# Neighbourhood attention with the two heads of a pair scored on the two row halves of TensorE, and a planner that groups by kind and knows PSUM banks

## The chip, the cores and the metric

The kernel runs on one core of one Trainium2 chip, in one launch. The metric is device time in microseconds (us). Three runs of the kernel before gave 2086.41, 2087.51 and 2084.97 us, a median of 2086.41.

## The reference, cut to what matters

Four layers work on 256 latent and 256 context tokens of width 1024. The layers' token mixers are grouped-query attention, neighbourhood attention, latent attention and grouped-query attention again; a SwiGLU feed-forward network with inner width 2816 follows each. All values are float32. The neighbourhood layer has 16 heads of 64 channels:

```python
q, k, v = jnp.split(t @ w_qkv, 3, axis=-1)          # shape (tokens, 16 heads, 64)
s_loc = einsum('bwhd,biwjhd->bhwij', qr, k_win) * scale + bias   # latent queries, latent keys in a window
s_ctx = einsum('bwhd,blhd->bhwl', qr, kc) * scale                # latent queries, all context keys
p = softmax(concatenate([s_loc, s_ctx], axis=-1))
o = einsum(p_loc, v_win) + einsum(p_ctx, vc)
oc = softmax_attend(qc, [kc], [vc], scale)          # context queries, context keys
```

Keys outside a window are masked by a bias of -1e30, so that all 256 latent keys are multiplied.

## The kernel before, in words

Every float32 product is made from float32r parts: an operand is split into a high part (ScalarE, ACT) and the rest (VectorE, DVE), and three TensorE matmuls add high*high, rest*high and high*rest into one PSUM bank. A weight piece of 128x1024 is loaded by SP, split into `whi` and `wlo`, and used. TensorE (PE) makes 128x512 or 128x256 outputs. PSUM has eight banks of 128x512, two for each of the tags `mm`, `sc`, `o` and `tp`.

Nothing is issued as it is written. Every call of the kernel is noted by `Planner.note` with a duration from `cost`; `schedule` then plays the program through in a list schedule, engine by engine, by due times from `backward`, and issues the instructions of the best of `PASSES` plans. So a planner's rule changes the order of the whole program. It knows the kind of a matmul, T (transpose), R (float32r) or F (other float32), and once it has issued a T it stays with T where it can.

In the neighbourhood layer (`attn_b`), `prep(c)` makes queries and keys of head pair c by two projections of 24 matmuls of 512 columns (tiles `m` = c and 8 + c, 128 channels = two heads), and for even c a quarter of the values. `stacked` takes each head apart: for a query, 64 rows of a tile `stk` hold the high part and the other 64 the rest; for a key, `stk` holds the high part in both halves and `stl` the rest in both. One head's scores are then two matmuls on all 128 rows, `ps<-stk` and `ps<-stl,stk`. That costs six ACT and six DVE instructions of 64x512 for a pair.

`head_units` gives three units for a head: context (`ca`: two blocks of 256 keys in one bank), and latent blocks 0 and 1 (`la`: 512 keys; the bias is added on DVE). A unit is scores, `softmax` (DVE maximum `nm`, ACT exponential `p`, DVE reciprocal `r`, POOL scaling `p`), then four transposes (`ps<-ident,p`) and their split (`pth`, `ptl`), then the product with `v`. `Pipe(2, 2)` sets these steps two units apart; `Stream` feeds the projections of the next pair between them.

`Norm.sums` makes the LayerNorm sums with 16 small F matmuls, each on 32 columns of the array (`ps<-zs,ones`, `ps<-x,ones`, `ps<-sq,ones`). `ada_first` and `ada_rest` multiply the modulation weights in the same way (`ps<-rawa,condp`).

Of the kernel before, what the change touches and what calls it, by code (L numbers as in the profile page):

```python
# [46 lines left out]
class Op:  # L47
    __slots__ = ("eng", "fn", "dur", "deps", "users", "tiles", "idx", "table", "left", "ready", "due", "start", "end",
                 "kind", "port", "rank", "pace")


class Planner:
# [9 lines left out]
    STAY = 1.5  # L62
    PASSES = 8
    PACE = 4.0
# [39 lines left out]
    def cost(self, queue, method, out, ins, k):  # L104
        n = 1
        for d in out.shape[1:]:
            n *= d
        if queue == "tensor":
            if method == "transpose":
                return 0.108  # L110
            if ins[0].dtype == F32R:
                return max(0.108, n / 2400.0 + 0.0133)
            return 0.083 if n <= 64 else 0.085 if n <= 128 else 0.242
        psum = any(x.space == bass.MemoryType.PSUM for x in ins)
        if queue == "sync":
            return n * out.shape[0] * 4 / 370e3
        n = max([n] + [self.width(x) for x in ins])
        extra = sum(self.width(x) == 1 for x in ins) + (k.get("accum_out") is not None)
        if queue == "scalar":
            return (0.05 if psum else 0.094) + n * 0.000835 + 0.093 * extra  # L120
        fast = method in ("tensor_scalar", "tensor_copy") and not psum
        if method == "reciprocal":
            return 0.07 + n * 0.0062
        if queue == "vector":
            return 0.07 + n * (0.00052 if fast else 0.00104) + 0.06 * extra
        if method == "tensor_scalar":
            return 0.115 + n * (0.00135 + 0.00035 * (len(ins) > 2))
        return 0.148 + n * 0.00217
# [18 lines left out]
    def note(self, queue, method, p, k):  # L147
# [16 lines left out]
        op.fn = lambda: getattr(getattr(self.nc, queue), method)(*p, **k)  # L164
        op.deps, op.users, op.tiles = set(), [], []
        for ap, w in [(x, False) for x in ins] + [(x, True) for x in outs]:
# [30 lines left out]
    def emit(self):  # L197
# [11 lines left out]
        for n in range(self.PASSES):  # L209
            self.backward(goal, aim)  # L210
            span = self.schedule()
            if best is None or span < best[0]:
                best = span, [o.start for o in self.ops]
            aim = [o.start if o.eng == "PE" else g for o, g in zip(self.ops, goal)]
        self.span, start = best
        for o in sorted(self.ops, key=lambda o: (start[o.idx], o.idx)):
            o.fn()
# [13 lines left out]
    def schedule(self):  # L231
# [15 lines left out]
        for o in ops:  # L247
            o.left = len(o.deps) + sum(slot[t] is None for t in o.tiles)
            o.ready = 0.0
            for t in o.tiles:  # L250
# [3 lines left out]

        def release(o, t):
            o.ready = max(o.ready, t)
            o.left -= 1
            if o.left == 0:
                heapq.heappush(engines[o.eng]["soon"], (o.ready, o.idx))
# [8 lines left out]
        port = 0.0  # L268
        kind = "R"
        while done < len(ops):  # L270
            best = None
# [11 lines left out]
            while e["soon"] and e["soon"][0][0] <= t:  # L283
                i = heapq.heappop(e["soon"])[1]
                heapq.heappush(e["ripe"], (prio(ops[i]), i))
            o = ops[e["ripe"][0][1]]
            if o.eng in ("DVE", "ACT", "POOL") and e["soon"]:
                urgent = [r for r, i in e["soon"] if r < t + o.dur - self.SLIP and ops[i].due < min(o.due, t + self.NEAR)]
                if urgent and o.due > t + self.SLACK:
                    r = min(urgent)  # L290
                    fit = [x for x in e["ripe"] if ops[x[1]].dur <= r - t + self.SLIP]
                    if not fit:
# [25 lines left out]
            if o.eng == "PE":  # L318
                if o.kind == "R" and kind != "R":
                    o.end += self.TURN  # L320
                kind = o.kind
            if o.port:
                port = o.end
            e["free"] = o.end
            done += 1
            for u in o.users:
                release(u, o.end + self.hop(o, u))
            for n in o.tiles:
# [59 lines left out]
def block_kernel(ctx: ExitStack, tc: tile.TileContext, a: dict, out: bass.AP):  # L388
# [381 lines left out]
    def head_units(qk, pv, evict, need, bias=None):  # L770
# [13 lines left out]

        def ca():
            ps = psum("sc")
            for b in range(2):
                qk(ps[:, b * 256:b * 256 + 256], slice(NL + b * P, NL + b * P + P), CTX)
            st["pc"] = softmax(ps, 2)
# [10 lines left out]

        def la(b):
            ps = psum("sc")
            qk(ps, slice(b * P, b * P + P), slice(0, T))
            if bias is not None:
# [17 lines left out]

        none = lambda: None
        us = [(lambda: la(0), lambda: lb(0), none), (lambda: la(1), lambda: lb(1), lc)]
        return ([(ca, cb, cc)] if need else []) + us

# [230 lines left out]

    def stacked(ps, sc, dup):


        res = []
        for s in range(2):
            r, o = slice(64 * s, 64 * s + 64), slice(64 - 64 * s, 128 - 64 * s)
            t = act("stk")
            if not dup:
                split_half(t, r, t, o, ps, r, sc)
                res.append(t)
            else:
                t2 = act("stl")
                nc.scalar.activation(t[r], ps[r], AF.Copy)  # L1070
                nc.scalar.activation(t[o], ps[r], AF.Copy)
                nc.vector.tensor_sub(t2[r], ps[r], f(t[r]))
                nc.vector.tensor_sub(t2[o], ps[r], f(t[r]))
                res.append((t, t2))
        return res

    def split_half(hi, rh, lo, rl, ps, r, sc):
        if sc is None:
            nc.scalar.activation(hi[rh], ps[r], AF.Copy)
            nc.vector.tensor_sub(lo[rl], ps[r], f(hi[rh]))  # L1080
        else:
            nc.scalar.activation(hi[rh], ps[r], AF.Copy, scale=sc)
            nc.vector.scalar_tensor_tensor(lo[rl], ps[r], sc, f(hi[rh]), op0=ALU.mult, op1=ALU.subtract)

    def attn_b(hh, hl, st):
# [24 lines left out]
        def prep(c):  # L1110
            if c % 2 == 0:
                yield from v_quarter(c // 2)
            for m in (c, 8 + c):
                wh, wl = load_w(key("b_qk", m))
                ps = psum("mm")
                yield from proj_feat(ps, wh, wl, 0, hh, hl, DC)
                QK[m] = stacked(ps, 0.125 if m < 8 else None, m >= 8)

        def first(st):
# [30 lines left out]
            for m, ps in zip((0, 8), pq):  # L1150
                QK[m] = stacked(ps, 0.125 if m < 8 else None, m >= 8)
            for kc in range(AHEAD, DC):
# [6 lines left out]

        def units(c, s):  # L1160
            def qk(ps, tq, tk):
                q, (kh, kl) = QK[c][s], QK[8 + c][s]
                nc.tensor.matmul(ps, q[:, tq], kh[:, tk], start=True, stop=False)
                nc.tensor.matmul(ps, q[:, tq], kl[:, tk], start=False, stop=True)

            c0 = ((c % 2) * 2 + s) * P
# [18 lines left out]

            return head_units(qk, pv, evict, True, bias)

        first(st)
        pipe = Pipe()
        flow = Stream(prep, [0] + [16 + (32 if c % 2 == 0 else 0) for c in range(1, 8)], 12, 0)  # L1190
        for c in range(8):
            flow.need(c)
            fill = flow.fill
            if c == 7:
                gen = (split_o(O, oh, ol, T, h, (nc.gpsimd, nc.vector)[h % 2]) for h in range(6))
                fill = filler(gen, 0.5)
            pipe.run(units(c, 0) + units(c, 1), fill)
        run(gen)
# [5 lines left out]
    def attn_c(hh, hl, st):  # L1204
# [96 lines left out]
        def qr_T(i):  # L1301
            tp = psum("tp")
            for tb in range(4):
                nc.tensor.transpose(tp[:, tb * P:tb * P + P], qr[tb][:, i * P:i * P + P], ident)
            QR[i] = stacked(tp, None, False)

# [294 lines left out]
```

## Time and profile before

| | kernel before |
|---|---|
| median of three runs | 2086.41 us |
| profiled execution | 2086.06 us |
| its span | 2083.9 us |
| PE busy | 2040.6 us |
| PE weight load busy | 1760.2 us |
| DVE, ACT, POOL busy | 1481.7, 961.9, 402.5 us |
| mean granted clock | 0.994 |

The span runs from the first to the last instruction; 2.16 us of the execution lie around it. The profile models the end of a matmul, so that neighbouring matmuls overlap in it: what a matmul takes of PE is read from the distance of two starts and not from its duration. Almost all instructions are issued by the planner and so have the same line (L164); they are told apart by the names of their tiles.

### The profile page before, as it was taken

How to read it: one execution, taken by the hardware profiler on the slowest of the kernel's cores; microseconds unless marked ns; L12 is line 12 of the kernel's file. 1: busy time of each engine (PE TensorE's matmuls, PEld its weight loads, DVE VectorE, ACT ScalarE, POOL GpSimd, SP SyncE). 2: the span in 40 equal slices, each digit the busy share in tenths (PEclk: the TensorE clock that was granted, in tenths of full speed). 3: DMA queues.
4: the chain of work that ended last, by engine and by line, in shares of the span. 5: the costliest groups of instructions: out<-in, count | busy, mean ns of one | idle time of the engine just before them, and what ended most of it. 6: DMA issues, size and time to landing. Idle time of an engine off the chain costs nothing.

```text
span 2083.9 us, 31923 instructions
## 1 busy us (share of the span) xinstructions
PE 2040.6 (98%) x12048; PEld 1760.2 (84%) x12048; DVE 1481.7 (71%) x2549; ACT 961.9 (46%) x1686; POOL 402.5 (19%) x508
## 2 busy tenths in 40 slices
PE   8999999999999999999999999999999999989997
PEld 4788988888888888988888898898888888789997
DVE  4687988786487776888786376659777755975554
ACT  4574722223386665722223386745222234766443
POOL 0334300000342234300000343251000005441002
PEclk9999999999999999999999999999999999999999
DMA  9424466665222212466555231126555642334552
GB/s 369 160 82 142 160 194 212 195 219 173 87 87 82 81 62 82 143 197 202 172 197 162 64 94 55 42 75 200 186 188 177 199 143 72 99 122 142 185 189 72
DMA packets 92121, 300.17 MB, mean 144 GB/s; under 512 B 11328, under 2 KB 11456, under 8 KB 91968
## 3 DMA queue, kind: packets, MB, share of 16 engines
q1 hardware_dynamic: 91968, 298.14, 44.0%
q8 instruction: 95, 1.56, 0.3%
q14 instruction: 58, 0.48, 0.1%
HBM read 297.05 MB, written 1.05 MB: 143 GB/s over the span
## 4 chain that ended last, share of the span: by engine, by line
PE 91%; ACT 3%; DVE 3%; DMA 1%; issue 1%; SPq 0%; POOL 0%; DVEq 0%; ACTq 0%; POOLq 0%
PE ps L164 91%; ACT stk L164 1%; ACT p L164 1%; DMA rawa<-in_w_ada 1%; DVE stl L164 1%; ACT whi L164 1%; DVE nm L164 1%; DMA raw<-in_a_wo 0%; ACT pth L164 0%; DVE junk L164 0%; ACT x L164 0%; DVE wlo L164 0%; SPq L164 0%; DVE ptl L164 0%; DVE x L164 0%
## 5 line engine op out<-in xcount | busy, mean ns | idle before, releaser
L164 ACT ACTIVATE whi<-raw 128x1024 fp32r<-128x1024 f32 (+3 forms) x371 | 379.7, 1028 | 714.0 <-PE ps L164 421.7
L164 PE MATMUL ps<-hh,whi 128*128 128x512 f32 (+1 forms) x1648 | 582.0, 355 | 1.7 <-ACT hh L164 1.7
L164 PE MATMUL ps<-hh,wlo 128*128 128x512 f32 (+1 forms) x1648 | 581.2, 353 | 0.0
L164 PE MATMUL ps<-hl,whi 128*128 128x512 f32 (+1 forms) x1648 | 580.8, 353 | 0.0
L164 DVE TENSOR_TENSOR wlo<-raw,whi 128x1024 fp32r<-128x1024 f32 (+3 forms) x359 | 442.5, 1237 | 110.4 <-ACT whi L164 107.4
L164 DVE SCALAR_TENSOR_TENSOR junk<-raw,sil 128x1024 bf16<-128x1024 f32 x320 | 392.3, 1226 | 126.4 <-DMA raw<-in_w_ada 123.6
L164 PEld LDWEIGHTS ps<-hh,whi 128*128 128x128 f32 x1648 | 312.3, 190 | 42.8 <-ACT hh L164 1.9
L164 PEld LDWEIGHTS ps<-hh,wlo 128*128 128x128 f32 x1648 | 312.7, 190 | 42.0
L164 PEld LDWEIGHTS ps<-hl,whi 128*128 128x128 f32 x1648 | 312.8, 190 | 40.9
L164 PE MATMUL ps<-gh,whi 128*128 128x512 f32 (+1 forms) x800 | 271.9, 341 | 0.0
L164 PE MATMUL ps<-gh,wlo 128*128 128x512 f32 (+1 forms) x800 | 271.7, 341 | 0.0
L164 PE MATMUL ps<-gl,whi 128*128 128x512 f32 (+1 forms) x800 | 271.6, 340 | 0.0
L164 DVE SCALAR_TENSOR_TENSOR x<-ps,G,x 128x256 f32<-128x256 f32 x224 | 102.2, 480 | 131.8 <-PE ps L164 131.4
L164 POOL TENSOR_TENSOR zs<-x,x 128x256 f32<-128x256 f32 x14 | 12.2, 873 | 844.4 <-DVE x L164 844.4
L164 PEld LDWEIGHTS ps<-gh,whi 128*128 128x128 f32 x800 | 151.5, 190 | 17.3
L164 PEld LDWEIGHTS ps<-gh,wlo 128*128 128x128 f32 x800 | 151.4, 190 | 17.0
L164 PEld LDWEIGHTS ps<-gl,whi 128*128 128x128 f32 x800 | 151.5, 190 | 17.0
L164 POOL TENSOR_SCALAR p<-p,r 128x512 f32<-128x512 f32 (+1 forms) x144 | 91.3, 641 | 271.7 <-DVE r L164 253.4
L164 PE MATMUL ps<-whi,hh 128*128 128x512 f32 (+3 forms) x352 | 124.1, 353 | 1.1 <-DVE v L164 1.1
L164 PE MATMUL ps<-wlo,hh 128*128 128x512 f32 (+3 forms) x352 | 120.7, 344 | 0.0
L164 PE MATMUL ps<-whi,hl 128*128 128x512 f32 (+3 forms) x352 | 119.7, 344 | 0.0
L164 PE MATMUL ps<-oh,whi 128*128 128x256 f32 (+1 forms) x352 | 108.7, 315 | 0.5 <-ACT p L164 0.3
(205 smaller groups left out, 3102.9 us busy)
## 6 DMA issues: line engine op xcount, KB each, us to landing
raw<-in_w_gu SPq DMA_DIRECT2D x176, 512.0 KB, 4.2
raw<-in_w_ada SPq DMA_DIRECT2D x160, 512.0 KB, 4.0
raw<-in_w_d SPq DMA_DIRECT2D x64, 448.0 KB, 4.0
rawa<-in_w_ada SPq DMA_DIRECT2D x64, 256.0 KB, 5.6
raw<-in_w_d SPq DMA_DIRECT2D x32, 512.0 KB, 3.7
raw<-in_a_qkv SPq DMA_DIRECT2D x24, 512.0 KB, 4.1
raw<-in_a_wo SPq DMA_DIRECT2D x16, 512.0 KB, 3.5
raw<-in_b_qk SPq DMA_DIRECT2D x16, 512.0 KB, 3.3
```

The costliest lines, as they stand in the source:

```text
L164: op.fn = lambda: getattr(getattr(self.nc, queue), method)(*p, **k)
```

## The change

Queries and keys are split once, over all 128 rows, into `qkh` and `qkl`. `units(c)` makes both heads' scores together: three matmuls for each head, on 64 rows, the heads alternating between rows 0 to 63 and rows 64 to 127 and writing two banks. The softmax and the rest of both heads follow unit by unit, with `Pipe(1, 1)`, and `Stream` has 6 slots for a pair in place of 12, since a pair now has half as many units. The planner gets a cost for 64-row matmuls and two others, stays with F as it stays with T, prefers on PE an instruction whose inputs have been there for `CALM` us, keeps ACT and DVE from one PSUM bank at the same time, and makes 16 passes. Uses of `stacked` in the latent attention stay as they were.

```diff
-    PASSES = 8
+    PASSES = 16
+    CALM = 0.3
...
-                return max(0.108, n / 2400.0 + 0.0133)
-            return 0.083 if n <= 64 else 0.085 if n <= 128 else 0.242
+                return max(0.108, n / 2400.0 + 0.0133) * (0.53 if ins[0].shape[0] == 64 else 1.0)
+            return 0.083 if n <= 64 else 0.06 if n <= 128 else 0.242
...
-            return n * out.shape[0] * 4 / 370e3
+            return n * out.shape[0] * 4 / 357e3
...
+            if ap.space == bass.MemoryType.PSUM and op.eng in ("ACT", "DVE"):
+                op.banks.append(t.name)
...
+            free = max([held[n][0] for n in o.banks if n in held and held[n][1] != o.eng], default=0.0)
+            if free > t:
+                heapq.heappop(e["ripe"])
+                heapq.heappush(e["soon"], (free, o.idx))
+                continue
...
-            if o.eng == "PE" and kind == "T" and o.kind == "R":
-                more = [x for x in e["ripe"] if ops[x[1]].kind == "T" and x[0] < o.rank + self.STAY]
+            if o.eng == "PE" and o.fresh > t - self.CALM:
+                calm = [x for x in e["ripe"] if ops[x[1]].fresh <= t - self.CALM]
+                if calm:
+                    x = min(calm)
...
+            if o.eng == "PE" and kind in ("T", "F") and o.kind != kind:
+                more = [x for x in e["ripe"] if ops[x[1]].kind == kind and x[0] < o.rank + self.STAY]
...
-                QK[m] = stacked(ps, 0.125 if m < 8 else None, m >= 8)
+                QK[m] = qk_out(m, ps)
+
+        def qk_out(m, ps):
+            th, tl = act("qkh"), act("qkl")
+            split_ps(th, tl, ps, imm=0.125 if m < 8 else None)
+            return th, tl
...
-        def units(c, s):
-            def qk(ps, tq, tk):
-                q, (kh, kl) = QK[c][s], QK[8 + c][s]
-                nc.tensor.matmul(ps, q[:, tq], kh[:, tk], start=True, stop=False)
-                nc.tensor.matmul(ps, q[:, tq], kl[:, tk], start=False, stop=True)
...
+            def scores(i):
+                (qh, ql), (kh, kl) = QK[c], QK[8 + c]
+                pss = [psum("sc") for _ in range(2)]
+                for b in range(2) if i == 0 else (0,):
+                    tq = slice(NL + b * P, NL + b * P + P) if i == 0 else slice((i - 1) * P, i * P)
+                    tk = CTX if i == 0 else slice(0, T)
+                    for k, (x, y) in enumerate(((qh, kh), (qh, kl), (ql, kh))):
+                        for s, ps in enumerate(pss):
+                            r = slice(64 * s, 64 * s + 64)
+                            o = ps[:, b * 256:b * 256 + 256] if i == 0 else ps
+                            nc.tensor.matmul(o, x[r, tq], y[r, tk], start=k == 0, stop=k == 2)
+                for ps, us in zip(pss, heads):
+                    us[i][0](ps)
...
-        pipe = Pipe()
-        flow = Stream(prep, [0] + [16 + (32 if c % 2 == 0 else 0) for c in range(1, 8)], 12, 0)
+        pipe = Pipe(1, 1)
+        flow = Stream(prep, [0] + [16 + (32 if c % 2 == 0 else 0) for c in range(1, 8)], 6, 0)
```

The order on PE, at the step from head pair 0 to head pair 1. Before, `ps_1216` is the key projection of pair 1 at its end, `ps_1247` the context scores of its first head, and `ps_1246` the value projection:

```order
L164 MATMUL ps_1216<-hh7_1112,wlo_1153 128x512
L164 MATMUL ps_1235<-ident_78,p_1208 128x128 x4
...
L164 MATMUL ps_1246<-whi_1189,hh3_1108 128x256
L164 MATMUL ps_1247<-stk_1236,stk_1211 128x256
...
L164 MATMUL ps_1254<-ident_78,p_1223 128x128 x4
L164 MATMUL ps_1246<-whi_1214,hh4_1109 128x256
L164 MATMUL ps_1247<-stl_1237,stk_1211 128x256
```

Transposes and value projections lie between the key projection and the two scores, the one that reads `stk` and the one that reads `stl`. After, on the same engine and at the same step, `ps_1218` is that key projection, and `ps_1246` and `ps_1247` are the context scores of the two heads:

```order
L165 MATMUL ps_1218<-hh7_1112,wlo_1153 128x512
...
L165 MATMUL ps_1236<-ptcl_1211,v_1172 128x256
...
L165 MATMUL ps_1246<-qkh_1237,qkh_1213 128x256
L165 MATMUL ps_1247<-qkh_1237,qkh_1213 128x256
L165 MATMUL ps_1245<-wlo_1193,hh1_1106 128x256
...
L165 MATMUL ps_1246<-qkl_1238,qkh_1213 128x256
L165 MATMUL ps_1247<-qkl_1238,qkh_1213 128x256
```

Behind the key projection now stand matmuls of the context product (`ptch`, `ptcl`) and of the value projection, and the scores come as neighbours for two heads, those that read `qkl` of the key seven rows behind the first. On PE a little later, the first latent block of the same pair has its two heads (`ps_1259`, `ps_1260`) apart:

```order
L165 MATMUL ps_1259<-qkh_1237,qkh_1213 128x512
L165 MATMUL ps_1259<-qkl_1238,qkh_1213 128x512
...
L165 MATMUL ps_1259<-qkh_1237,qkl_1214 128x512
L165 MATMUL ps_1272<-whi_1192,hl0_1113 128x256
...
L165 MATMUL ps_1260<-qkh_1237,qkh_1213 128x512
L165 MATMUL ps_1260<-qkl_1238,qkh_1213 128x512
```

Here the second head's three matmuls come 26 rows after the first head's last. The order on PE before, at the LayerNorm sums (`ps_2292`) at the start of the latent layer, beside its projection (`ps_2287`, `ps_2288`):

```order
L164 MATMUL ps_2292<-zs_2214,ones_83 32x64 x2
L164 MATMUL ps_2287<-wlo_2239,hh1_2250 128x320
L164 MATMUL ps_2292<-zs_2214,ones_83 32x64 x2
L164 MATMUL ps_2287<-whi_2238,hl1_2258 128x320
L164 MATMUL ps_2292<-x7_107,ones_83 32x64 x2
L164 MATMUL ps_2288<-whi_2238,hh0_2249 128x320
L164 MATMUL ps_2292<-x7_107,ones_83 32x64
```

Runs of two or fewer sums alternate with projection matmuls. The same place on PE after (`ps_2276` the sums):

```order
L165 MATMUL ps_2276<-zs_2198,ones_83 32x64 x4
L165 MATMUL ps_2271<-wlo_2223,hh1_2234 128x320
L165 MATMUL ps_2271<-whi_2222,hl1_2242 128x320
L165 MATMUL ps_2276<-x7_107,ones_83 32x64 x4
L165 MATMUL ps_2276<-sq_2197,ones_83 32x64 x4
L165 MATMUL ps_2276<-sq_2265,ones_83 32x64 x4
```

The 16 sums stood in nine runs between projection matmuls and now stand in two.

## Rows read from the trace of the kernel before

**Rows 1.** The page: busy time of each engine, and the chain by engine.

```profile
PE 2040.6 (98%) x12048; PEld 1760.2 (84%) x12048; DVE 1481.7 (71%) x2549; ACT 961.9 (46%) x1686; POOL 402.5 (19%) x508
...
PE 91%; ACT 3%; DVE 3%; DMA 1%; issue 1%; SPq 0%; POOL 0%; DVEq 0%; ACTq 0%; POOLq 0%
```

**Rows 2.** Stretches: start, end, length, busy (count) by engine, clock, DMA share.

```profile
100.00:200.00 100.00, 96.23 (x620) 80.42 (x619) 84.10 (x160) 63.86 (x134) 40.49 (x58) 1.00 0.33 111
300.00:500.00 200.00, 200.00 (x884) 165.61 (x883) 166.45 (x256) 52.66 (x62) 0.00 (x0) 1.00 0.66 207
595.00:797.00 202.00, 193.13 (x1196) 167.94 (x1195) 151.90 (x267) 140.77 (x296) 58.96 (x73) 1.00 0.21 71
1800.00:1868.00 68.00, 64.20 (x446) 58.24 (x445) 55.05 (x101) 44.91 (x90) 27.77 (x39) 0.97 0.23 76
```

**Rows 3.** PE in time order: start, duration, instruction, count.

```profile
644.85 0.28 PE L164 MATMUL ps<-ptcl,v 128*128 128x256 f32 x1
644.97 0.28 PE L164 MATMUL ps<-ptch,v 128*128 128x256 f32 x1
...
649.10 0.60 PE L164 MATMUL ps<-ident,p 128*128 128x128 f32 x4
649.45 0.47 PE L164 MATMUL ps<-hh,whi 128*128 128x512 f32 x1
649.76 0.39 PE L164 MATMUL ps<-hl,whi 128*128 128x512 f32 x1
```

**Rows 4.** Groups by shape, 595 to 797 us: busy, mean ns, idle before, releaser.

```profile
L164 ACT ACTIVATE stk<-ps 64x512 fp32r<-64x512 f32 x48 | 28.3, 592 | 21.4 <-PE ps L164 15.0 <-DVE stl L164 6.0
L164 DVE TENSOR_TENSOR stl<-ps,stk 64x512 fp32r<-64x512 f32 x32 | 22.0, 688 | 14.0 <-ACT stk L164 13.7
L164 DVE TENSOR_REDUCE nm<-ps 128x1 f32<-128x512 f32 x31 | 21.4, 689 | 0.9
L164 ACT ACTIVATE p<-ps,nm 128x512 f32<-128x512 f32 x31 | 21.3, 689 | 27.3 <-DVE nm L164 20.4 <-PE ps L164 6.4 <-issue 0.3
L164 DVE TENSOR_TENSOR ps<-ps,bias 128x256 f32<-128x256 f32 x32 | 13.6, 425 | 8.9 <-PE ps L164 8.8
```

**Rows 5.** Waits of PE and its weight load, 595 to 797 us: total, times, longest.

```profile
PEld ps L164 <- DVE stl L164: 6.8, 6, 1.5
PEld ps L164 <- ACT p L164: 3.0, 5, 1.1
PEld ps L164 <- ACT stk L164: 0.9, 1, 0.9
PE ps L164 <- DVE stl L164: 4.8, 6, 1.1
```

**Rows 6.** All engines in time order, at a step between head pairs.

```profile
651.80 1.20 ACT L164 ACTIVATE stk<-ps 64x512 fp32r<-64x512 f32 x2 [1.47 <-PE ps L164]
653.03 0.68 DVE L164 TENSOR_TENSOR stl<-ps,stk 64x512 fp32r<-64x512 f32 x1 [1.97 <-ACT stk L164]
655.11 0.39 PE L164 MATMUL ps<-stl,stk 128*128 128x256 f32 x1 [0.96 <-DVE stl L164]
```

**Rows 7.** PE in time order, where F matmuls stand between float32r ones.

```profile
202.14 0.26 PE L164 MATMUL ps<-zs,ones 128*32 128x64 f32 x3
...
202.72 0.39 PE L164 MATMUL ps<-oh,whi 128*128 128x256 f32 x1
...
1205.76 0.31 PE L164 MATMUL ps<-whi,hl 128*128 128x320 f32 x1
1205.91 0.31 PE L164 MATMUL ps<-whi,hh 128*128 128x320 f32 x1
...
1206.38 0.41 PE L164 MATMUL ps<-wlo,hh 128*128 128x320 f32 x1
1206.72 0.31 PE L164 MATMUL ps<-zs,ones 128*32 128x64 f32 x4
1206.96 0.41 PE L164 MATMUL ps<-whi,hl 128*128 128x320 f32 x1
```

More of the change, by code (lines that the diff above doesn't have):

```diff
@@ L48 @@
     __slots__ = ("eng", "fn", "dur", "deps", "users", "tiles", "idx", "table", "left", "ready", "due", "start", "end",
-                 "kind", "port", "rank", "pace")
+                 "kind", "port", "rank", "pace", "banks", "fresh")
 class Planner:
@@ L165, in note @@
         op.deps, op.users, op.tiles = set(), [], []
+        op.banks = []
         for ap, w in [(x, False) for x in ins] + [(x, True) for x in outs]:
@@ L212, in emit @@
             if best is None or span < best[0]:
-                best = span, [o.start for o in self.ops]
+                best = span, [(o.start, o.end) for o in self.ops]
             aim = [o.start if o.eng == "PE" else g for o, g in zip(self.ops, goal)]
         self.span, start = best
-        for o in sorted(self.ops, key=lambda o: (start[o.idx], o.idx)):
+        for o in self.ops:
+            o.start, o.end = start[o.idx]
+        for o in sorted(self.ops, key=lambda o: (o.start, o.idx)):
             o.fn()
@@ L248, in schedule @@
             o.left = len(o.deps) + sum(slot[t] is None for t in o.tiles)
-            o.ready = 0.0
+            o.ready = o.fresh = 0.0
             for t in o.tiles:
@@ L253, in schedule, with release @@
         last = {t: 0.0 for t in uses}
-        def release(o, t):
+        def release(o, t, own=False):
             o.ready = max(o.ready, t)
+            if not own:
+                o.fresh = max(o.fresh, t)
             o.left -= 1
@@ L269, in schedule @@
         kind = "R"
+        held = {}
         while done < len(ops):
@@ L290, in schedule @@
                     r = min(urgent)
-                    fit = [x for x in e["ripe"] if ops[x[1]].dur <= r - t + self.SLIP]
+                    fit = [x for x in e["ripe"] if ops[x[1]].dur <= r - t + self.SLIP and not ops[x[1]].banks]
                     if not fit:
@@ L302, in schedule @@
                 heapq.heappop(e["ripe"])
-            if o.eng == "PE" and kind == "T" and o.kind == "R":
-                more = [x for x in e["ripe"] if ops[x[1]].kind == "T" and x[0] < o.rank + self.STAY]
+            if o.eng == "PE" and o.fresh > t - self.CALM:
+                calm = [x for x in e["ripe"] if ops[x[1]].fresh <= t - self.CALM]
+                if calm:
+                    x = min(calm)
+                    e["ripe"].remove(x)
+                    e["ripe"].append((o.rank, o.idx))
+                    heapq.heapify(e["ripe"])
+                    o = ops[x[1]]
+            if o.eng == "PE" and kind in ("T", "F") and o.kind != kind:
+                more = [x for x in e["ripe"] if ops[x[1]].kind == kind and x[0] < o.rank + self.STAY]
                 if more:
@@ L318, in schedule @@
             if o.eng == "PE":
-                if o.kind == "R" and kind != "R":
+                if o.kind != kind and (kind != "R" or o.kind == "F"):
                     o.end += self.TURN
@@ L323, in schedule @@
                 port = o.end
+            for n in o.banks:
+                held[n] = o.end + self.FROM[o.eng], o.eng
             e["free"] = o.end
@@ L326, in schedule @@
             for u in o.users:
-                release(u, o.end + self.hop(o, u))
+                release(u, o.end + self.hop(o, u), u.eng == o.eng)
             for n in o.tiles:
@@ L783, in out_ps, with ca @@
             return st["o"]
[L785 to L788, printed above, removed]
+        def ca(ps=None):
+            if ps is None:
+                ps = psum("sc")
+                for b in range(2):
+                    qk(ps[:, b * 256:b * 256 + 256], slice(NL + b * P, NL + b * P + P), CTX)
             st["pc"] = softmax(ps, 2)
@@ L799, in cc, with la @@
                 pv(o[:, CTX], 2 + i, v[0][:, :, i, :], v[1][:, :, i, :], i == 0, i == 1)
-        def la(b):
-            ps = psum("sc")
-            qk(ps, slice(b * P, b * P + P), slice(0, T))
+        def la(b, ps=None):
+            if ps is None:
+                ps = psum("sc")
+                qk(ps, slice(b * P, b * P + P), slice(0, T))
             if bias is not None:
@@ L823, in head_units @@
         none = lambda: None
-        us = [(lambda: la(0), lambda: lb(0), none), (lambda: la(1), lambda: lb(1), lc)]
+        us = [(lambda ps=None: la(0, ps), lambda: lb(0), none), (lambda ps=None: la(1, ps), lambda: lb(1), lc)]
         return ([(ca, cb, cc)] if need else []) + us
@@ L1056, in attn_a, with stacked @@
         return oh, ol
-    def stacked(ps, sc, dup):
+    def stacked(ps):
         res = []
@@ L1064, in stacked @@
             t = act("stk")
[L1065 to L1074, printed above, removed]
-        return res
[L1077 to L1083, printed above, removed]
+            nc.scalar.activation(t[r], ps[r], AF.Copy)
+            nc.vector.tensor_sub(t[o], ps[r], f(t[r]))
+            res.append(t)
+        return res
     def attn_b(hh, hl, st):
@@ L1150, in first @@
             for m, ps in zip((0, 8), pq):
-                QK[m] = stacked(ps, 0.125 if m < 8 else None, m >= 8)
+                QK[m] = qk_out(m, ps)
             for kc in range(AHEAD, DC):
@@ L1158, in attn_b, with head @@
         oh, ol = [], []
-        def units(c, s):
-            def qk(ps, tq, tk):
-                q, (kh, kl) = QK[c][s], QK[8 + c][s]
-                nc.tensor.matmul(ps, q[:, tq], kh[:, tk], start=True, stop=False)
-                nc.tensor.matmul(ps, q[:, tq], kl[:, tk], start=False, stop=True)
+        def head(c, s):
             c0 = ((c % 2) * 2 + s) * P
@@ L1184, in evict, with units, both @@
                 nc.vector.tensor_add(O[c][r], o[r], t[r])
-            return head_units(qk, pv, evict, True, bias)
+            return head_units(None, pv, evict, True, bias)
+        def units(c):
+            heads = [head(c, s) for s in range(2)]
+            def scores(i):
[11 more added lines that the diff above has]
+                    us[i][0](ps)
+            def both(i, k):
+                for us in heads:
+                    us[i][k]()
+            return [(lambda i=i: scores(i), lambda i=i: both(i, 1), lambda i=i: both(i, 2)) for i in range(3)]
         first(st)
-        pipe = Pipe()
-        flow = Stream(prep, [0] + [16 + (32 if c % 2 == 0 else 0) for c in range(1, 8)], 12, 0)
+        pipe = Pipe(1, 1)
+        flow = Stream(prep, [0] + [16 + (32 if c % 2 == 0 else 0) for c in range(1, 8)], 6, 0)
         for c in range(8):
@@ L1195, in attn_b @@
                 gen = (split_o(O, oh, ol, T, h, (nc.gpsimd, nc.vector)[h % 2]) for h in range(6))
-                fill = filler(gen, 0.5)
-            pipe.run(units(c, 0) + units(c, 1), fill)
+                fill = filler(gen, 1.0)
+            pipe.run(units(c), fill)
         run(gen)
@@ L1304, in qr_T @@
                 nc.tensor.transpose(tp[:, tb * P:tb * P + P], qr[tb][:, i * P:i * P + P], ident)
-            QR[i] = stacked(tp, None, False)
+            QR[i] = stacked(tp)
         def units(h):
```

## The prediction

> **What bounds the kernel now.** I read the page first, then a table of stretches, then the waits in the neighbourhood layer, then PE in time order. The page shows PE busy for 98% of the span and 91% of the chain on PE [rows 1]: a microsecond less PE work, or less waiting by PE, is a microsecond off the end, and work taken off DVE or ACT is worth only the PE wait that it ends. The stretches show where PE waits at all [rows 2]. In the feed-forward network (300 to 500 us) it never does: 884 matmuls in 200 us, one every 0.226 us, which I take as the price of a 512-column matmul. In the first grouped-query attention PE lacks 3.8 of 100 us, in the neighbourhood layer 8.9 of 202, in the last attention 3.8 of 68. These three stretches and the order of PE's own instructions are all that the change can reach.
>
> More prices come from PE in time order. A 256-column matmul takes 0.12 us from start to start (644.85 to 644.97), and four transposes take 0.35; the float32r matmul behind them takes 0.31 in place of 0.226, so that the turn from T to R costs 0.084 [rows 3].
>
> **Scores.** Before, the layer has 64 score matmuls of 256 columns and 64 of 512: 64 x 0.12 + 64 x 0.226 = 22.1 us. After, it has 96 of each, on 64 rows. The new order on PE has 43 neighbouring pairs and 10 single ones of 256 columns, and 30 pairs and 36 singles of 512. The singles come from the second score bank not being free in the plan. If a pair runs in the time of one, that is 53 x 0.12 + 66 x 0.226 = 21.3 us: 0.9 saved, not the quarter that three matmuls in place of four suggest. If the halves do not overlap it is 96 x 0.12 + 96 x 0.226 = 33.2, or 11.1 lost. No row before shows row halves, but 15 sums on 32-column quarters take 0.58 us in all (202.14 to 202.72), 0.039 each [rows 7], far less than any matmul on its own, so that parts of the array do work side by side. I take the overlap.
>
> A pair of 256 columns needs two weight loads in the time of one matmul. Below, they cost nothing; above, the two run one behind the other, 43 x 0.12 = 5.2 us. The nearest row are the transposes, each with its own load and few columns, 0.35 / 4 = 0.0875: 43 x (2 x 0.0875 - 0.12) = 2.4 us lost, and I take that. The Trainium skill, page "TensorE: Matmul & The Clock Gate", section "LDWEIGHTS (loading the stationary operand)", says that a load's time goes by its columns and not by its rows, 128 columns at 1.2 per ns; by that a pair needs 0.213 us, and the loss would be an estimated 4.0 us.
>
> PE goes from 128 rows to row halves and back 42 times. A change of shape without a change of type is in no row. Below it costs nothing. Above stands the entry into column quarters, which changes type as well: one projection matmul and two sums (each has two records) take 1206.38 to 1206.96 = 0.58 us, the matmul alone 0.15 (1205.76 to 1205.91) and two sums in a run 0.08, so that an entry costs 0.35 [rows 7]. The turn behind a transpose, 0.084, changes only type, and I take it as the nearer: 42 x 0.084 = 3.5 us lost (0 to 14.7).
>
> **Splitting queries and keys.** Gone are 48 ACT and 48 DVE instructions of 64x512 at 0.59 and 0.69 us; 16 of each come, over 128 rows, at the same price for an instruction. That takes 19 us from ACT and 22 from DVE [rows 4], hidden, since both have slack in the layer (141 and 152 of 202 us busy [rows 2]). What counts is the chain behind the last key matmul. ACT starts at 651.80, two halves take 1.20, DVE takes 0.68 at 653.03, then ACT waits for DVE on the same bank, and the score that needs `stl` starts at 655.11, PE having been idle 0.96 [rows 6]. With one ACT and one DVE instruction the rest is there at about 651.80 + 0.59 + 0.69 = 653.1, two microseconds earlier, and the new order has more filler before that score. So the waits on `stl` go: PE lost between 4.8 (idle PE) and 6.8 + 0.9 (weight load idle for `stl` and `stk`) [rows 5]. I take 6.5. Next latest are the weight loads that wait for the exponential, 3.0 us [rows 5], which stay.
>
> **F and T kept together.** The order has 33 entries into the LayerNorm sums before and 18 after: seven fewer at the start of the latent layer, where the price of 0.35 was read, 2.5 us, and eight fewer elsewhere, one sum having been split off each time. For those I take the middle of 0.084 and 0.35, 1.8. Entries into transposes fall from 137 to 116: 21 x 0.084 = 1.8. Entries into the modulation matmuls fall from 29 to 18, early on where PE waits in any case: at the lower price, 0.9 (0 to 3.9).
>
> **The rest of the planner.** The counts of all other instructions are the same. DMA order on SP hardly moves, and the feed-forward network, where weights flow fastest, keeps its order and its full PE. The new DMA rate, `CALM`, the banks and the further passes reorder the four attention stages; I give that zero, with the rival below for more. `Pipe(1, 1)` and both heads at once lengthen the last pair's tail, where output-projection matmuls fill PE as before: zero, with a rival for the other sign.
>
> **Sum.** 4.3 (sums) + 1.8 (transposes) + 0.9 (modulation) + 6.5 (waits) + 0.9 (scores) - 2.4 (loads) - 3.5 (shape) = 8.5 us. The profiled execution took 2086.06 us, 2.16 of it around the span and not touched, and lies 0.35 under the median of the runs shown: 2086.06 - 8.5 = 2077.6, on the scale of the median 2077.9.
>
> **Rivals.**
>
> *More in other stages.* Knowing banks and preferring settled inputs could end half of what PE still lacks: 3.8 + 3.8 + (8.9 - 5.5) = 11.0 [rows 2, 5], half is 5.5: 2072.4. For it: ACT stands 6.0 us before `stk` alone for DVE on the same bank [rows 4], which the old plan did not foresee. Against it: the waits of the last attention sit on chains that an order can't shorten.
>
> *The halves do not overlap.* The change then doesn't do what it says. 4.3 + 1.8 + 0.9 + 6.5 - 11.1 - 3.5 = -1.1: 2087.5. For it: nothing before has run on row halves. Against it: the column quarters.
>
> *Every change of shape empties the array.* At 0.35 for each of 42 runs the sum is 8.5 + 3.5 - 14.7 = -2.7: 2089.1. For it: a projection matmul that follows sums loses most of that price [rows 7]. Against it: half of that may be the change of type, which a transpose's 0.084 [rows 3] shows to be smaller. The Trainium skill, page "TensorEngine Tiling (Array Packing)", section "Tiling Modes", says that changing the tiling mode, as against the tile, drains TensorE; this is the rule by which this rival would hold, and the sums agree with it in sign.
>
> *Two banks held by two softmaxes (slower).* Both score banks now fill together, 24 times, and PE can't make the next scores until both exponentials are through. The second head's bias, maximum and exponential are 0.43 + 0.69 + 0.69 = 1.8 us [rows 4]. If half of it stands in front of PE in each unit, 24 x 0.9 = 21.6 us: 2099.5. It turns the result slower by more than 4.2 from (8.5 + 4.2) / 24 = 0.53 us a unit. For it: the 36 single scores, and 3.0 us already lost on exponentials [rows 5]. Against it: every pair but the last brings 48 projection matmuls, 10.9 us, to run in between.
>
> **How the numbers follow.** Forecast 0.50, more elsewhere 0.17, no overlap 0.11, emptied array 0.13, held banks 0.09. The likeliest own range is 2072 to 2083, from the bounds of entries, loads and waits. With every price at its good end the sum is 5.2 + 1.8 + 3.9 + 7.7 + 0.9 = 19.5, 2066.9; that is the low end. The high end, 2087, leaves out the emptied array at full price, the held banks and half of the missing overlap. A measurement of this kernel can tell 0.2%, 4.2 us: faster is below 2082.2, slower above 2090.6. Faster holds nearly all of the first two cases and the milder part of the third and fourth, 0.70; the same most of the third and fourth, 0.20; slower the held banks and a rest, 0.10.
>
> **What would show it.** Row halves: starts of a pair a few ns apart, and a 512-column pair over in about 0.23 us. Loads: 256-column pairs 0.175 apart, not 0.12. Shape: the full matmul behind a half one at 0.31 or less, not 0.5. Splitting: no wait of PE on `qkl` over 0.3 us at the steps between pairs. Sums: two runs in place of nine at the latent layer, over some 2.5 us sooner. Feed-forward stretches at 0.226 a matmul as before. It would be wrong if PE lacked more than 9 us in the neighbourhood layer, or if score matmuls took over 26 us from start to start.

## The result, and the profile after

The kernel after takes 2072.61 us (median of four runs, 2070.77 to 2073.35) against 2086.76 for the kernel before beside it: a ratio of 0.9932, interval 0.9915 to 0.9949. That is 14.2 us sooner, where 8.5 were forecast. The profiled execution, at 2073.35 us the slowest of its four, is 12.7 us under that of before, and the accounts below go by it.

PE's part of the chain rises, and its busy time falls by 3 us only (after, busy time by engine and the chain, as in [rows 1]):

```profile
PE 2037.4 (98%) x12112; PEld 1756.1 (85%) x12112; DVE 1456.2 (70%) x2517; ACT 936.2 (45%) x1654; POOL 410.3 (20%) x508
...
PE 95%; DVE 3%; ACT 1%; DMA 1%; issue 0%; POOL 0%; SPq 0%; DVEq 0%; ACTq 0%; POOLq 0%
```

Three stretches of after that answer to [rows 2], with the same columns (start, end, length, then busy time and count of PE, its weight load, DVE, ACT and POOL, the clock, the DMA share, GB/s):

```profile
100.00:200.00 100.00, 97.14 (x669) 82.83 (x668) 82.45 (x157) 60.80 (x131) 48.65 (x57) 1.00 0.33 106
300.00:500.00 200.00, 200.00 (x884) 165.66 (x883) 168.60 (x269) 52.93 (x63) 0.00 (x0) 1.00 0.65 207
595.00:797.00 202.00, 200.62 (x1231) 164.15 (x1231) 126.80 (x239) 118.52 (x265) 55.25 (x73) 1.00 0.22 71
```

The feed-forward network has 884 matmuls in 200 us as before. In the neighbourhood layer PE lacks 1.4 us where it lacked 8.9, and DVE and ACT have lost 25 and 22 us of work. From this alone the layer should be 7.5 us shorter. It is not. In the table a stage runs from the first LayerNorm-sum matmul of one sublayer to that of the next, worked out from the starts of PE's matmuls in each profiled execution, in us. The first attention begins with the first matmul of the kernel, and the last feed-forward network ends with the end of the last one. The kernels below the first two are the experiments.

| kernel | first attention | neighbourhood | latent | last attention | four feed-forward |
|---|---|---|---|---|---|
| before | 197.8 | 263.9 | 190.4 | 118.9 | 1301.1 |
| after | 192.0 | 265.8 | 186.5 | 115.1 | 1300.1 |
| old layer, new planner | 192.7 | 257.7 | 186.5 | 116.8 | 1298.8 |
| new layer, old planner | 198.6 | 261.0 | 190.6 | 116.2 | 1300.7 |
| before, stay with F | 192.6 | 264.0 | 187.5 | 115.3 | 1299.9 |
| after, not staying with F | 195.9 | 263.7 | 189.9 | 116.6 | 1301.2 |
| after, halves grouped | 192.4 | 256.2 | 186.4 | 116.6 | 1300.1 |
| after, halves scattered | 191.9 | 285.9 | 186.6 | 115.2 | 1299.0 |
| after, no `CALM` | 193.5 | 268.6 | 186.9 | 115.7 | 1298.5 |
| after, full price | 191.5 | 262.8 | 186.4 | 118.8 | 1299.4 |

The neighbourhood layer became 1.9 us longer; the gain lies in the three other attention stages (5.8, 3.9 and 3.8), and about 1 us in the feed-forward ones. What took the layer's gain back stands in PE's own order. After, a run of context scores (start, duration, instruction, count; x2 are the two heads, whose starts mostly lie 3 or 4 ns apart):

```profile
595.79 0.28 PE L165 MATMUL ps<-wlo,hh 128*128 128x256 f32 x1
595.91 0.28 PE L165 MATMUL ps<-whi,hl 128*128 128x256 f32 x1
596.12 0.39 PE L165 MATMUL ps<-qkh 64*128 64x256 f32 x2
596.34 0.28 PE L165 MATMUL ps<-qkl,qkh 64*128 64x256 f32 x2
596.46 0.28 PE L165 MATMUL ps<-qkh,qkl 64*128 64x256 f32 x2
...
596.81 0.28 PE L165 MATMUL ps<-qkh,qkl 64*128 64x256 f32 x2
597.02 0.50 PE L165 MATMUL ps<-hh,whi 128*128 128x512 f32 x1
597.36 0.40 PE L165 MATMUL ps<-hl,whi 128*128 128x512 f32 x1
597.60 0.39 PE L165 MATMUL ps<-hh,wlo 128*128 128x512 f32 x1
```

A pair costs 0.12 (596.34 to 596.46), as one full matmul does. But the last full matmul takes 0.21 in place of 0.12, the first pair 0.22, the last pair 0.21, and the first full one behind it 0.34 in place of 0.23: 0.09 + 0.10 + 0.09 + 0.11 = 0.39 us for a run of half-row matmuls. Summed over the layer, the half-row matmuls take 29.4 us from start to start. Their count gives 21.5 (53 pairs and singles of 256 columns at 0.117, 30 pairs of 512 at 0.235 and 36 singles at 0.23), so that 7.9 lie above it. The full matmuls next to them take 7.5 more than elsewhere. That makes 15.4 for 42 runs, 0.37 each. PE counts as busy through all of it. Only the weight load shows it, as idle time for which the profile has no releaser. The waits in the layer (568 to 830 us; total, times, longest) answer to [rows 5]:

```profile
PE ps L165 <- ACT p L165: 1.4, 1, 1.4
PE ps L165 <- POOL hl L165: 0.5, 1, 0.5
PEld ps L165 <- issue: 12.3, 38, 0.4
PEld ps L165 <- ACT p L165: 2.2, 2, 1.8
PEld ps L165 <- ACT pth L165: 1.2, 4, 0.4
```

No wait on `stl`, `stk` or `qkl` is left, and all 38 short waits put down to "issue" stand where the shape changes. The 42 runs have 84 such places, so that not each shows one.

### The profile page after: what moved, and what is told of

Read it like the earlier page. It is cut to its first block, busy times and chain, and to the rows that moved or that the text cites. A ratio compares the mean times of both kernels' runs of the same rounds, so it can differ in the third digit from the quotient of the medians.

```text
span 2071.6 us, 32014 instructions
## 1 busy us (share of the span) xinstructions
PE 2037.4 (98%) x12112; PEld 1756.1 (85%) x12112; DVE 1456.2 (70%) x2517; ACT 936.2 (45%) x1654; POOL 410.3 (20%) x508
## 4 chain that ended last, share of the span: by engine, by line
PE 95%; DVE 3%; ACT 1%; DMA 1%; issue 0%; POOL 0%; SPq 0%; DVEq 0%; ACTq 0%; POOLq 0%
PE ps L165 95%; DVE x L165 1%; DVE wlo L165 0%; ACT p L165 0%; DVE nm L165 0%; DMA bada<-in_b_ada 0%; DMA rawa<-in_w_ada 0%; POOL sq L165 0%; DVE junk L165 0%; SPq L165 0%; DVE ql L165 0%; DVE h L165 0%; DVE R L165 0%; ACT L165 0%; DVE ptl L165 0%
## 5 line engine op out<-in xcount | busy, mean ns | idle before, releaser
L165 DVE TENSOR_TENSOR wlo<-raw,whi 128x1024 fp32r<-128x1024 f32 (+3 forms) x359 | 439.5, 1228 | 120.5 <-ACT whi L165 118.9
L165 POOL TENSOR_SCALAR p<-p,r 128x512 f32<-128x512 f32 (+1 forms) x144 | 95.6, 673 | 250.9 <-DVE r L165 230.3
L165 ACT ACTIVATE p<-ps,nm 128x512 f32<-128x512 f32 (+1 forms) x144 | 84.4, 592 | 64.0 <-DVE nm L165 60.8
```

## The experiments

**The two halves of the change, each alone.** The neighbourhood layer of before under the planner of after (`stacked_b` is the `stacked` of before, and the units, the 12 slots of `Stream` and the score matmuls are those of before too):

```diff
-                QK[m] = qk_out(m, ps)
+                QK[m] = stacked_b(ps, 0.125 if m < 8 else None, m >= 8)
...
-        pipe = Pipe(1, 1)
+        pipe = Pipe()
```

> The planner of the kernel after with the neighbourhood layer of the kernel before (heads stacked, scores on 128 rows). Theory A: the gain of 14.2 us comes from the planner's rules in all attention stages, and in the neighbourhood layer the changes of shape (about 0.39 us for each of 42 runs, 16 us) eat what the shorter split chain gives. Then this kernel keeps the gains outside the layer and its layer takes no longer than the 263.9 us of before, minus under 4 us for fewer turns: 2066 to 2072. Theory B: the gain comes from the layer's new split and its row halves, and the rest is small: 2080 to 2086.

2066.66 us, 0.9903 of before (0.9888 to 0.9918), in the range of theory A. And the layer of after under the planner of before (with its `PASSES`, costs and `schedule`):

```diff
-            if o.eng == "PE" and kind in ("T", "F") and o.kind != kind:
+            if o.eng == "PE" and kind == "T" and o.kind == "R":
```

> The neighbourhood layer of the kernel after with the planner of the kernel before (8 passes, full price for 64-row matmuls, no rule for F, banks or settled inputs). Theory A: the three other attention stages are as before (197.8, 190.4 and 118.9 us) and the layer is 0 to 5 us longer than the 263.9 of before: 2086 to 2092. Theory B: 2072 to 2078.

2080.79 us, 0.9969 (0.9956 to 0.9981), between the two theories' ranges and in neither: the layer became shorter and the last attention 2.7 us shorter, where theory A had the one longer and the other as before. So the planner alone gives 20.1 us, the layer alone 6.0, and both together 14.2, 6 us less than the planner alone. Of the 8.1 us by which the layer is longer after than with the old layer under the new planner, the shape changes would be 15.4; the rest is fewer waits and turns. Under the old planner the layer has 36 runs of half-row matmuls in place of 42 and fewer singles, and gains 2.9 on the old one. Under the new planner the old layer has lost half of its waits as well (the weight load's, without "issue", fell from 15.7 to 7.9 us), so that less is left to win.

**The halves grouped.** Half-row matmuls become a kind of their own, H, with which PE stays as with T and F; the score that needs both rests comes first, and the first matmul of a unit waits in the plan until both banks are free, so that no head goes alone. Within a run the plan takes the other row half next, and it counts 0.19 us for a turn to or from H.

```diff
-            op.kind = "T" if method == "transpose" else "R" if ins[0].dtype == F32R else "F"
+            op.kind = ("T" if method == "transpose" else "F" if ins[0].dtype != F32R else
+                       "H" if ins[0].shape[0] == 64 else "R")
...
-            if o.eng == "PE" and kind in ("T", "F") and o.kind != kind:
+            if o.eng == "PE" and kind in ("T", "F", "H") and o.kind != kind:
...
-                    for k, (x, y) in enumerate(((qh, kh), (qh, kl), (ql, kh))):
+                    for k, (x, y) in enumerate(((ql, kh), (qh, kl), (qh, kh))):
```

> The kernel after, with the 64-row matmuls as a kind of their own (H) that the planner stays with, the products with the rest first (so that a run starts when all its inputs are there) and a run started only when both score banks are free. On PE 28 runs of row halves in place of 42, and all 96 pairs neighbours. If a change of shape costs 0.39 us a run, the runs give 14 x 0.39 = 5.5 us and the 18 latent and 5 context pairs that now overlap give 18 x 0.23 + 5 x 0.12 = 4.7 us: 10 us off, 2062 to 2066. If the lost time around the runs is waiting for inputs and not the change of shape, the runs give nothing and only the overlap shows: 2068 to 2070. If waiting for both banks costs PE what the grouping gives: 2071 to 2075.

2064.38 us, 0.9893 (0.9879 to 0.9908): faster than both kernels, and in the range for a price of 0.39 us a run. The order has 28 runs and 96 neighbouring pairs, and the layer is 9.6 us shorter than after's. 14 runs at 0.39 and the singles that became pairs (18 x 0.235 + 5 x 0.117 = 4.8) make 10.3.

**The halves scattered.** The same kernel, but PE leaves the half-row matmuls for a ready full one after each pair, and no longer stays with H.

```diff
-            if o.eng == "PE" and kind in ("T", "F", "H") and o.kind != kind:
+            if o.eng == "PE" and kind in ("T", "F") and o.kind != kind:
...
-            if o.eng == "PE" and kind == "H":
+            if o.eng == "PE" and kind == "H" and half == 64:
+                more = [x for x in e["ripe"] if ops[x[1]].kind == "R"]
...
+            elif o.eng == "PE" and kind == "H":
```

> The kernel of halves_grouped (all 96 pairs are neighbours) in which TensorE leaves the half-row matmuls for a ready full-row one after each pair: 94 runs of half-row matmuls in place of 28, nothing else moved by intent. Theory A, each run of half-row matmuls costs about 0.39 us in and out: 66 x 0.39 = 25.7 us over the 2064.4 of halves_grouped, 2087 to 2092. Rival B, the price of the forecast, 0.084 us a run: 5.5 us over, 2069 to 2071. Rival C, a change of shape costs nothing and grouping gained by the pairs alone: 2063 to 2067.

2092.56 us, 1.0027 of before (1.0017 to 1.0038): 28.2 over the grouped kernel, or 0.43 for each of the 66 added runs and 0.6 over the upper end of theory A. Not all of it is the runs. PE's own waits in the layer are 1.3 us longer (2.6 against 1.3), and behind the longest of them, 1.5 us, the granted clock is at the lower of its two levels (1.2 and 2.4 GHz) for 3.4 us; seven matmuls of 512 columns take 0.43 each there in place of 0.23, some 1.4 us. Without both, 25.5 us are left, 0.39 a run. The price of a run holds; 0.084 and zero are out. It also turns the change from faster to slower with the same instructions. Its order on PE:

```profile
596.77 0.39 PE L167 MATMUL ps<-qkl,qkh 64*128 64x256 f32 x2
597.09 0.50 PE L167 MATMUL ps<-hh,whi 128*128 128x512 f32 x1
597.52 0.39 PE L167 MATMUL ps<-qkh 64*128 64x256 f32 x2
597.83 0.51 PE L167 MATMUL ps<-hl,whi 128*128 128x512 f32 x1
598.27 0.38 PE L167 MATMUL ps<-qkh,qkl 64*128 64x256 f32 x2
```

A full matmul between two pairs takes 0.43 (597.09 to 597.52) in place of 0.227, and a lone pair 0.31 (597.52 to 597.83) in place of 0.12. The stretch from 595 to 797 us, scattered and then grouped, shows how little "busy" says of it:

```profile
595.00:797.00 202.00, 202.00 (x1141) 153.99 (x1140) 113.11 (x213) 103.75 (x235) 50.29 (x65) 1.00 0.21 68
```

```profile
595.00:797.00 202.00, 201.27 (x1288) 169.71 (x1287) 130.25 (x244) 121.62 (x270) 56.80 (x73) 1.00 0.24 79
```

PE is busy for all of 202.00 us in the slower kernel, with 1141 matmuls; in the faster one 1288 fit into the same time. The weight load's waits on "issue" in that stretch go with the runs (94 and 28 in the whole layer): 90 and 23 of them.

```profile
PEld ps L167 <- issue: 22.0, 90, 0.4
```

```profile
PEld ps L167 <- issue: 7.8, 23, 0.4
```

**Staying with F.** The rule taken out of after, with its turn:

```diff
-            if o.eng == "PE" and kind in ("T", "F") and o.kind != kind:
+            if o.eng == "PE" and kind == "T" and o.kind == "R":
...
-                if o.kind != kind and (kind != "R" or o.kind == "F"):
+                if o.kind == "R" and kind != "R":
```

> The kernel after without the rule that PE stays with F matmuls (and without the turn's price in front of F): 36 entries into the LayerNorm sums in place of 18, and 25 into the modulation matmuls in place of 18. By the price of 0.35 us an entry read before: 18 x 0.35 = 6.3 and 7 x 0.08 to 0.35 = 0.6 to 2.5 us lost, 2079 to 2082. If the sums cost little (0.08 each): 2074 to 2076.

2081.03 us, 0.9973 (0.9963 to 0.9984), in the range for 0.35 us an entry: 8.4 of the 14.2 us are gone. Up to 1.7 of them may be the granted clock, which in the profiled execution is at its lower level for 3.4 us in the first attention. The same two places, the other way round, as the only change to before:

> The kernel before with one rule added: PE stays with F matmuls as with T, and the turn's price also stands in front of F. Entries into the LayerNorm sums fall from 33 to 19, into the modulation matmuls from 29 to 17. If the taking away of this rule (8.4 us lost) measured its own worth, this kernel gains 14 x 0.35 = 4.9 us and 12 x 0.08 to 0.35 = 1 to 4 us: 2077 to 2081. If its worth comes only with the other rules: 2084 to 2087.

2073.68 us, 0.9937 (0.9922 to 0.9951), faster than either range expected: this one rule gives 12.5 us by itself, where 5 to 9 were expected. In the table its three other attention stages stand within about 1 us of after's, while its neighbourhood layer stands as before. Modulation entries on PE fall from 29 to 17 and those into the sums from 33 to 19. At the second set of sums in the latent layer it has the order that after has.

**The other rules of the planner**, each taken out of after alone.

```diff
-    CALM = 0.3
+    CALM = -1e9
```

> The kernel after without the rule that PE prefers settled inputs. On PE it has 48 runs of row halves in place of 42. If the rule ends waits of PE in the attention stages: at least 3 us lost there, and 6 x 0.39 = 2.3 us for the runs, 2077 to 2081. If the gain outside the layer is that of F and T kept together alone: only the runs show, 2073 to 2076.

2076.41 us, 0.9947 (0.9931 to 0.9964), 3.8 over after and between the two ranges; 2.8 of it in the neighbourhood layer, which has 48 runs of half-row matmuls in place of 42, 2.3 us at 0.39. The three other attention stages lose 2.5 us together, and the feed-forward ones win 1.6.

```diff
-                op.banks.append(t.name)
+                pass
```

> The kernel after with a planner that doesn't know that ACT and DVE can't use one PSUM bank at the same time. 42 runs of row halves as after. If planned bank conflicts were what the old planner lacked: 2 to 5 us lost in the attention stages, 2075 to 2078. If PE has enough other work in front of it: no difference, 2071 to 2075.

2072.45 us, 0.9932 (0.9917 to 0.9946), in the second range: the banks give nothing that can be told from after.

```diff
-                return max(0.108, n / 2400.0 + 0.0133) * (0.53 if ins[0].shape[0] == 64 else 1.0)
+                return max(0.108, n / 2400.0 + 0.0133)
```

> The kernel after, the planner's price of a 64-row matmul being that of a 128-row one in place of 0.53 of it. 38 runs of row halves in place of 42, 45 pairs of 256 columns in place of 43, and as many singles of 512. By 0.39 us a run: 1.6 us and 0.2 us gained, 2070 to 2072. If the half price is what made the layer slow, it goes back to the 261.0 us that the layer takes under the old planner: 2067 to 2069.

2072.29 us, 0.9931 (0.9916 to 0.9945): the same time as after, 0.3 over the first range, and made up otherwise. The layer is 2.9 us shorter, with 38 runs in place of 42. The last attention is 3.7 longer, although it has no 64-row matmul whose price could change: a rule moves the order everywhere, so that one stage can win or lose some 4 us by the way. What a single rule gives in a stage that it doesn't name can't be told from that by one run.

**A longer stay**, in the grouped kernel:

```diff
-    STAY = 1.5
+    STAY = 3.0
```

> The kernel of halves_grouped in which the planner lets TensorE stay with its kind of matmul for 3.0 us in place of 1.5: entries into transposes 115 to 107, into modulation 18 to 14, into the sums 16 to 15. Theory A, entries are what is left to save: 8 x 0.084 + 4 x 0.43 + 0.35 = 2.7 us sooner than halves_grouped, 2060.5 to 2063. Rival B, what waits behind the longer stay costs as much as the entries save: 2064 to 2068.

2063.87 us, 0.9887 (0.9871 to 0.9904), not to be told from the grouped kernel's 2064.38 and 0.1 under the range of rival B. The entries fell as planned, but the first attention became 1.4 us longer (193.8 against 192.4). Whether that is what rival B says, that something behind the longer runs was needed sooner, was not looked into.

## Why the prediction was right, and which of its terms were not

The side and the range held, and so did the mechanism of most terms. That the time came out only 5.3 us under the forecast is in part luck: the largest term was wrong by 11.9 us, and several smaller ones were wrong the other way. By the forecast's terms the neighbourhood layer itself was to become shorter, by 1.5 us even without the transposes; it became 1.9 longer. One of the prediction's own signs of being wrong came, too: score matmuls of over 26 us from start to start (29.4).

*Overlap of the halves* held: two starts a few ns apart, a pair of 512 columns over in 0.235 us. So did the count by which the scores save almost nothing: 0.6 us, where 0.9 was forecast.

*Loads of 256-column pairs*: 2.4 us were forecast as lost, at 0.175 a pair; a pair takes 0.117. The term is zero, its lower bound. The estimate of 0.213 put two loads one behind the other, each at the price that the Trainium skill, page "TensorE: Matmul & The Clock Gate", section "LDWEIGHTS (loading the stationary operand)", gives for a load; two loads into different row halves don't add up so here.

*Change of shape* is the step that failed: "The turn behind a transpose, 0.084, changes only type, and I take it as the nearer: 42 x 0.084 = 3.5 us lost (0 to 14.7)." It cost 15.4, 0.37 to 0.39 a run, just past the upper bound, and it does so without a change of type. The full matmul behind a run takes 0.34, over the 0.31 that was named as the sign. The rival by which every change of shape empties the array had the price about right (0.35). The Trainium skill, page "TensorEngine Tiling (Array Packing)", section "Tiling Modes", has the rule, a drain when the tiling mode changes, and the four lengthened matmuls of each run agree with it. That an emptied array is the reason is argued from this rule; what the runs show is the price and its place. The rival's time of 2089.1 came out some 16 us too late because it kept the forecast's other terms: modulation (4.0 more, at the same price), waits (3.4), transposes (1.4), loads (2.4) and the stages given zero (4.8) all came out better.

*Modulation entries* were priced by the same wrong row: 11 x 0.084 = 0.9, because PE was thought to wait there in any case. It does not: in the kernel before PE is busy for all of the 30 us from 20 to 50 us. The price could have been read there, where full matmuls and 32-column ones alternate:

```profile
31.13 0.39 PE L164 MATMUL ps<-wlo,hh 128*128 128x512 f32 x1
31.36 0.40 PE L164 MATMUL ps<-whi,hl 128*128 128x512 f32 x1
31.68 0.42 PE L164 MATMUL ps<-rawa,condp 128*32 128x128 f32 x8
32.04 0.50 PE L164 MATMUL ps<-whi,hh 128*128 128x512 f32 x1
32.38 0.40 PE L164 MATMUL ps<-wlo,hh 128*128 128x512 f32 x1
```

The full matmul ahead takes 0.32 and the one behind 0.34, in place of 0.23: 0.2 on the full side alone, as at the row halves. The first attention became 5.8 us shorter; PE's waits in it fell only from 12.4 to 11.5, so that 4.9 remain for 11 entries, 0.45 each, as an estimate. The kernel before with the rule for F alone agrees: 12 entries fewer, and 5.2 us less in that stage. The idle time ahead of the modulation's matmuls and weight loads, by what ended it (total, times), before and then after, very nearly counts the entries, at 0.32 to 0.34 each:

```profile
  DMA rawa<-in_w_ada: 20.4, 20
  issue: 8.9, 28
```

```profile
  DMA rawa<-in_w_ada: 16.2, 19
  issue: 5.1, 15
```

*Sums* held. In after's latent layer, in answer to [rows 7]:

```profile
1201.58 0.31 PE L165 MATMUL ps<-whi,hh 128*128 128x320 f32 x1
1201.82 0.32 PE L165 MATMUL ps<-zs,ones 128*32 128x64 f32 x8
1202.07 0.41 PE L165 MATMUL ps<-wlo,hh 128*128 128x320 f32 x1
1202.32 0.30 PE L165 MATMUL ps<-whi,hl 128*128 128x320 f32 x1
1202.56 0.32 PE L165 MATMUL ps<-x,ones 128*32 128x64 f32 x8
1202.69 0.41 PE L165 MATMUL ps<-sq,ones 128*32 128x64 f32 x16
1203.03 0.41 PE L165 MATMUL ps<-whi,hh 128*128 128x320 f32 x1
```

Two runs in place of nine. The set takes 1.21 us with two projection matmuls in it, 0.91 without them; before it took 3.7 without its eight. That is 2.8 against 2.5 forecast; the whole stage became 3.9 shorter. What the other eight entries gave (1.8 forecast) was not measured by itself.

*Waits*: 6.5 were forecast for `stl` and `stk`, and all of them went. In total the weight load's waits in the layer, without "issue", fell from 15.7 to 5.8, by 9.9, since those on the exponential and on `v` shrank as well. *Transposes*: the full float32r matmuls right behind transposes fell from 52 to 24 in the layer, and what they took above the price of their size from 5.4 to 2.2 us, by 3.2, against 1.8 forecast. For the layer this makes - 9.9 (waits) - 3.2 (transposes) + 15.4 (shape) - 0.6 (scores) = + 1.7, where + 1.9 was measured; terms under 1 us each are left out.

*Other stages by reordering*: zero was forecast. The last attention gave 3.8. Around its last wait on the exponential, before and after:

```profile
1800.00:1824.00 24.00, 20.32 (x102) 15.98 (x101) 20.27 (x43) 14.67 (x31) 10.13 (x19) 0.93 0.07 23
```

```profile
1789.00:1813.00 24.00, 22.22 (x120) 17.86 (x119) 22.34 (x47) 15.62 (x34) 14.96 (x23) 1.00 0.14 48
```

PE's longest wait there fell from 2.6 to 0.8 us, and all its waits in the stage from 3.6 to 1.9, which is 1.7. Behind the longest wait the granted clock of before is at its lower level for 3.4 us, and in after it stays at the full one. Before, at the end of that wait:

```profile
1811.67 0.79 PE L164 MATMUL ps<-kh,qh 128*128 128x512 f32 x1 [2.56 <-ACT p L164]
1812.27 0.63 PE L164 MATMUL ps<-kl,qh 128*128 128x512 f32 x1
1812.69 0.63 PE L164 MATMUL ps<-kh,ql 128*128 128x512 f32 x1
```

Six such matmuls start 0.43 apart (the first 0.60) in place of 0.23, some 1.3 us. So the wait and the clock make 3.0 of the 3.8. Two more kernels, both with the planner's rules of after, have a wait of 2.6 us there and a clock that falls for 3.4 us: the old layer under the new planner (116.8) and the full price (118.8). This stretch of the full price shows it:

```profile
1786.00:1810.00 24.00, 19.62 (x96) 15.77 (x95) 19.25 (x41) 13.73 (x30) 12.21 (x20) 0.93 0.10 35
```

These three are the longest in this stage; the other kernels take 114.9 to 116.6. So its gain goes with whether the order happens to have that wait, and no rule of the planner is shown to end it: here the result was helped by luck. The total falls on the time of the rival *More in other stages* (2072.4), but not for its reasons: knowing the banks gave nothing, and `CALM` gave its 3.8 us mostly in the neighbourhood layer.

*Two banks held by two softmaxes* didn't come: PE waits once on an exponential in the layer, for 1.4 us.

Staying with F alone also gives almost all of after's gain in the last attention (115.3). It has PE's longest wait there at 1.3 us and no fall of the clock; why that order avoids the longer wait stays open.

## What to carry to other kernels

Price a change of TensorE's shape apart from a change of type: here about 0.4 us for each run of row-half or column-quarter matmuls between full ones, against 0.084 for a turn from transposes. Make the runs long before counting on the overlap, and let the planner know the kind: here that made of a layer 1.9 us longer than before one 7.7 us shorter. PE's busy share does not show this cost; count matmuls in equal stretches, and look at the weight load's waits on "issue". And try each half of a change alone: here one half gave more than the whole.

## What the runs showed of the hardware that was not expected

Two matmuls on different row halves mostly start 3 or 4 ns apart, and even at 256 columns their two weight loads cost nothing (0.117 us a pair). Entering and leaving row halves costs as much as entering and leaving 32-column quarters (0.2 us on the full side for both), although the first changes no type.
